# First expert layer: experts sorted by token count on the chip and packed into 14 units of 128 slots

## The chip, the cores and the metric

The kernel runs on one core of a Trainium2 chip. The metric is the device time of one execution in microseconds (us). TensorE (PE) does the matmuls, VectorE (DVE), ScalarE (ACT) and GpSimd (POOL) the elementwise work, and SyncE (SP) issues nearly all transfers. All arithmetic shown here is in f32 or, split into a high and a low part, in fp32r.

## The reference

The program is a block of two transformer layers on 256 latent and 256 context tokens of width 1024, followed by a second block. Each of the two layers ends in a mixture of 32 experts, of which every token takes two. The change touches the first layer's mixture alone, with 512 tokens and so 1024 (token, expert) pairs. Cut to what matters:

```
grp   = argmax(h @ w_group + b_group)                 # one of 4 groups
top_i = the 2 best of the 8 experts of that group
gate  = p_group * softmax over the two
counts[e] = how many tokens take expert e
y[t]  = sum over its two experts e of
        gate * ((silu(h[t] @ w1[e]) * (h[t] @ w3[e])) @ w2[e])
```

w1[e] and w3[e] are 1024 x 512, w2[e] is 512 x 1024, all f32: 2 MiB each, 6 MiB an expert, 192 MiB a layer. The result must not depend on how tokens are laid out for the experts.

## The kernel before, in words

`moe(l, Tn, ob)` is the mixture of layer l over Tn tiles of 128 tokens (4 in the first layer). It routes, ranks each token inside its expert (`pk`), and gives it a slot: `slot = 64 * expert + rank`. Tokens with a rank of 64 or more (`ovr`) go to slots behind `OVF` = 2048.

The main loop at the end of `moe` goes through 16 units of 128 slots, each two experts with 64 slots. For a unit it does, on TensorE: on every second unit `gather` (the tokens of two units are picked by one-hot matrices from `onehot_tok` into `xt`, 8 x 256 columns), `up` with w1 (L1155: for each of 8 rows of weights, one matmul for each expert, 64 stationary columns of `xt` and 512 moving columns of the weight), `trans` of the unit before, `up` with w3, `down` of the unit before (L1190), and `combine` of the unit before (L1217: the result is scattered back to the tokens by one-hot matrices from `scatter_mats` and added to X). An f32 matmul is two matmul instructions, two passes over its 512 columns. Two matmuls with 64 stationary columns, one for each expert of a unit, lie side by side in the array.

Weights come as tiles of 1 MiB through a ring of eleven buffers (`Stream`, `W.load`, L259). One expert is six tiles, the layer 192. The order is that of use: w1 and w3 of unit i+1 before w2 of unit i. SP issues each load as soon as the tile eleven places ahead has been used. The first four experts have fixed places (`FIX`); the number of each of the other 28 is read by SP from the tile `eid` (`Q.value_load`, L820), because places can be swapped at run time.

The swap: `overflow_slots` counts the tokens of each expert (L1101) and works out which have more than 64; `swap` puts one such expert into place 15, the second expert of unit `px` = 7, and unit 7 carries an extra set of 128 slots for its tokens behind the 64th. For this, `up` and `down` take `extra`: each row of that expert's weights is also multiplied with 128 more columns (L1158, L1194); `gather(onehot_tok(swap_base()), 128)` fetches the tokens, and the set has its own `trans`, `scaled` and `combine` (`late`). If more is left, `overflow_loop` (L1265 on) runs a loop with a trip count known only at run time; each trip loads one expert and does 128 slots, with nothing beside it. The branch stands after unit 14.

On the inputs that are used the counts of the first layer, by expert, are 10, 35, 25, 26, 21, 15, 45, 31, 32, 23, 26, 37, 32, 27, 31, 22, 40, 62, 42, 48, 29, 65, 29, 43, 28, 26, 34, 35, 20, 26, 18, 41. Expert 21 has one token more than 64.

Instructions are placed by the tile framework's scheduler, which goes by data dependences and the order in which they are written; on each engine the order is then fixed.

Behind the layer comes the attention of the second layer (its first TensorE work is L397); the modulation projections, spread over several stages, use four matmuls of 32 stationary columns side by side (L314).

Of the kernel before, what the change touches and what calls it, by code (L numbers as in the profile page):

```python
# [19 lines left out]
NE = 32  # L20
# [5 lines left out]
SLOT_FREE = -1.0e6  # L26


def _consts():
# [19 lines left out]
    put("w8", np.broadcast_to((8 - np.arange(8))[None, :], (128, 8)))  # L49
    put("half", np.stack([p < 64, p >= 64], 1))  # L50
# [75 lines left out]
def build(tc, A, out, stages=("A0", "M0", "A1", "M1", "F", "B"), dbg=None, inject=None):  # L126
# [22 lines left out]
    with es:  # L149
# [40 lines left out]
        def C(name):  # L190
            a, b = C1COLS[name]
            return c1[:, a:b]
# [575 lines left out]
        def moe(l, Tn, ob):  # L768
            N = 128 * Tn
            nC = Tn // 2  # L770
            nj = (N - CAP + 127) // 128
# [41 lines left out]
            nP = NE // 2  # L813
            order = list(range(nP))
            px = 7 if l == 0 else None
            dyn = {}

            def sources(i):
                if i not in dyn:
                    ids = [e if l or e < FIX else Q.value_load(eid[0:1, e:e + 1], min_val=0, max_val=NE - 1) for e in (2 * i, 2 * i + 1)]  # L820
                    dyn[i] = list(zip(*map(expert, ids)))
                return dyn[i]

            ws = {}
            for p, i in enumerate(order + [None]):
                if i is not None:
                    ws[i] = [stream.add(lambda i=i, j=j: sources(i)[j], 2, 8, 4) for j in range(2)]
                if p:
                    b = order[p - 1]
                    ws[b].append(stream.add(lambda b=b: sources(b)[2], 2, 4, 2))  # L830
# [8 lines left out]
            with sbuf(f"ringx{l}", nX, "right") as ringX, ExitStack() as mid, ExitStack() as early, ExitStack() as main:  # L839
# [235 lines left out]
                has = sm(1)  # L1075
                V.memset(has, 0.0)
                if l == 0:
                    eid = lbx[:, 0:32].bitcast(I32)

                def swap():  # L1080
                    it, sw = C("iota32"), t2(M_)
                    hs, hd, e15 = (sw[:, 32 * i:32 * i + 32] for i in range(3))
                    dsum = sw[:, 96:97]
                    q = 2 * px + 1
                    V.tensor_scalar(hs, it, float(FIX), None, op0=OP.is_ge)
                    V.scalar_tensor_tensor(hs, ovb[:, 0], 0.0, hs, op0=OP.is_equal, op1=OP.mult)
                    V.scalar_tensor_tensor(hs, ovb[:, 1], 0.0, hs, op0=OP.is_gt, op1=OP.mult, accum_out=has)
                    V.tensor_scalar(hd, it, -1.0, float(q), op0=OP.mult, op1=OP.add)
                    V.scalar_tensor_tensor(hd, hd, 1.0, hs, op0=OP.mult, op1=OP.mult, accum_out=dsum)
                    V.tensor_scalar(e15, it, float(q), dsum, op0=OP.is_equal, op1=OP.mult)  # L1090
                    V.tensor_add(hd, hd, it)
                    V.tensor_sub(hd, hd, e15)
                    V.tensor_copy(eid[0:1], hd[0:1])
                    pick(ek, hd[:, None, None, :].to_broadcast(wide))
                    V.tensor_scalar(ek, ek, float(CAP), None, op0=OP.mult)
                    V.tensor_add(slot, ek, pk)

                def overflow_slots():
                    pc = PS()
                    for t in range(Tn):  # L1100
                        T.matmul(pc[0:32, 0:2], at_[:, t], C("ones")[:, 0:2], start=(t == 0), stop=(t == Tn - 1))  # L1101
                    V.tensor_copy(cntc[0:32], pc[0:32, 0:1])
                    for j in range(nj):
                        V.tensor_scalar(cmp_[0:32, j:j + 1], cntc[0:32], float(CAP + 128 * j), None, op0=OP.is_gt)
                    V.tensor_reduce(ovc[0:32], cmp_[0:32], axis=AX.X, op=OP.add)
                    yield
                    po = PS()
                    for i, m in enumerate(("tri", "ident", "ones")):
                        T.matmul(po[:, 32 * i:32 * i + 32], ovc[0:32].to_broadcast([32, 128]), C(m)[0:32, 0:32], start=True, stop=True)
                    V.tensor_copy(ovb, po[:, 0:96].rearrange("p (a b) -> p a b", a=3))  # L1110
                    V.tensor_sub(ovb[:, 0], ovb[:, 2], ovb[:, 0])
                    V.tensor_sub(ovb[:, 0], ovb[:, 0], ovb[:, 1])
                    if l == 0:
                        swap()
                    pick(bk, ovb[:, 0, None, None, :].to_broadcast(wide))
                    V.tensor_scalar(bk, bk, 128.0, float(OVF - CAP), op0=OP.mult, op1=OP.add)
# [30 lines left out]
                def up(off, ws, mid=lambda: None, extra=False):  # L1147
                    ps = PS()
                    px_ = PS() if extra else None
# [26 lines left out]
                def down(hT_, ws, gt, end=False, extra=None):  # L1176
# [10 lines left out]
                    for k in range(4):  # L1187
                        for jo, ps in enumerate(pss):
                            for q, w in enumerate(ws):
                                T.matmul(ps[m * q:m * q + m, :], hT_[:, k, m * q:m * q + m],  # L1190
                                         at(w, k)[k, slice(512 * jo, 512 * jo + 512)], start=(k == 0), stop=(k == 3))
                        if extra:
                            for jo, ps in enumerate(extra[1]):
                                T.matmul(ps, extra[0][:, k], w[k, slice(512 * jo, 512 * jo + 512)], start=(k == 0), stop=(k == 3))  # L1194
# [60 lines left out]
                def swap_base():  # L1255
                    sb = M_.tile([128, 1], F32, name="sb", tag="sb", bufs=1)
                    V.tensor_scalar(sb, has, -4.0 * OVF, 5.0 * OVF, op0=OP.mult, op1=OP.add)
                    return sb

                def overflow_loop():  # L1260
                    ctr = sm(1)
                    V.tensor_copy(ctr, has)
                    nb = M_.tile([1, 1], I32, name="nb")
                    V.tensor_scalar(nb, ovb[0:1, 2, 0:1], has[0:1], 0.0, op0=OP.subtract, op1=OP.max)
                    nbv = nc.values_load(nb[0:1, 0:1], min_val=0, max_val=2 * N // (CAP + 1))  # L1265
# [11 lines left out]
                pend = late = sr = gt = None  # L1277
                for i in order + [None]:
                    ext = i is not None and i == px
                    after = pend and pend[4]  # L1280
                    if i is not None:
# [3 lines left out]
                        if ext:  # L1285
                            gather(onehot_tok(swap_base()), 128)
# [6 lines left out]
                        if not late and i > 1:  # L1293
                            sr, gt = scatter_mats(swap_base() if after else 128 * i, i == order[-1])
                        if i != 0:
                            p1 = up(off, ws[i][0], extra=ext)
# [4 lines left out]
                        if late:  # L1301
                            combine(late[0], scaled(late[1], late[2]))
                            late = None
                            sr, gt = scatter_mats(128 * i)
                    tr = trans(pend[0]) if pend else None
                    if after:
                        xs = trans(after), [PS(), PS()]
                    if i:
                        p3 = up(off, ws[i][1], extra=ext)
                    if pend:  # L1310
                        ys = down(tr, pend[1], pend[2], i is None, xs if after else None)
                    if i is not None:
                        hx = act(p1[1], p3[1]) if ext else None
                        hd = act(p1[0], p3[0]) if ext else act(p1, p3)
# [4 lines left out]
                    if after:  # L1319
                        late = sr, xs[1], gt  # L1320
                        sr, gt = scatter_mats(128 * i)
                    pend = None if i is None else [hd, ws[i][2], gt, sr, hx]
# [762 lines left out]
```

## Time and profile before

| | us |
|---|---|
| median of three runs | 2151.06 (2144.14 to 2153.21) |
| span of the profiled execution | 2151.6 |
| TensorE busy in it | 2024.5 (94%) |
| DVE, ACT, POOL busy | 1131.6, 675.4, 511.6 |
| bytes moved | 585.43 MB, mean 272 GB/s |

The page gives no time of the profiled execution beside its span. Shares of busy time are means over stages with different limits: the two expert layers, attention, projections and the second block. What counts for a change in one stage is what bounds that stage.

### The profile page before, as it was taken

Reading aid. Unit: us, or ns where it says so; the run is one execution under the profiler, and the core shown is the slowest. Engines: PE = TensorE matmul, PEld = TensorE weight load, DVE = VectorE, ACT = ScalarE, POOL = GpSimd, SP = SyncE. Lnnn points to the kernel's source line nnn. Section 1 sums busy time; section 2 is a strip of 40 time slices with the busy share of each in tenths; the row PEclk is TensorE's granted clock in tenths of the full one; section 3 lists DMA queues with packets and bytes.
Section 4 is the critical chain, followed back from the end, with each engine's and each line's share of the span. In section 5 each row is a group of like instructions: output and inputs, shape, how many; then the busy total and the mean of one; then the engine's idle time right before and its main releaser. Section 6 shows DMA issues by size and latency. Waiting matters only on the chain. (4 is left out here: it accounts for less than half of the span.)

```text
span 2151.6 us, 29161 instructions
## 1 busy us (share of the span) xinstructions
PE 2024.5 (94%) x11233; PEld 1296.2 (60%) x11233; DVE 1131.6 (53%) x2024; ACT 675.4 (31%) x1220; POOL 511.6 (24%) x391
## 2 busy tenths in 40 slices
PE   6999989999999997999889999899989999997998
PEld 3755665445434543567754444343358998997996
DVE  3486574556355446764763333332365885455553
ACT  3365531101001111533731111110145344445553
POOL 1234321223222211420011111111113350242331
PEclk8999999999999999999999999899999999998999
DMA  9572358999689997744359999999964453554552
GB/s 316 210 254 102 98 195 328 419 419 398 235 330 371 421 413 283 256 168 155 119 221 415 424 424 423 388 424 424 424 255 138 137 187 120 193 179 140 184 194 98
DMA packets 154175, 585.43 MB, mean 272 GB/s; under 512 B 17256, under 2 KB 21862, under 8 KB 121134
## 3 DMA queue, kind: packets, MB, share of 16 engines
q1 hardware_dynamic: 153182, 583.48, 70.4%
q8 instruction: 91, 1.49, 0.3%
q14 instruction: 54, 0.44, 0.1%
q10 hardware_dynamic: 848, 0.01, 0.0%
HBM read 582.34 MB, written 1.11 MB: 271 GB/s over the span
## 5 line engine op out<-in xcount | busy, mean ns | idle before, releaser
L1155 PE MATMUL ps<-w,xt 128*64 128x512 f32 x1968 | 474.2, 605 | 16.8 <-DVE sid L1132 11.4
L1155 PEld LDWEIGHTS ps<-w,xt 128*64 128x64 f32 x1968 | 146.3, 139 | 286.8 <-issue 274.8
L1224 POOL TENSOR_TENSOR X<-X,tm 128x512 f32<-128x512 f32 x94 | 128.9, 1372 | 760.6 <-DVE tm L1223 754.8
L226 DVE TENSOR_TENSOR spl<-w,sph 128x1024 fp32r<-128x1024 f32 (+1 forms) x153 | 203.1, 1330 | 197.5 <-ACT sph L223 196.5
L223 ACT CAST sph<-w 128x1024 fp32r<-128x1024 f32 (+1 forms) x204 | 213.0, 1045 | 286.2 <-PE pj L217 255.0
L1208 DVE SCALAR_TENSOR_TENSOR t<-ps,gt,t 128x512 fp32r<-128x512 f32 x62 | 46.5, 751 | 471.9 <-ACT t L1207 469.7
L1190 PE MATMUL ps<-w,t 128*64 128x512 f32 x1000 | 242.6, 596 | 6.5 <-DMA w<-expert_w 5.2
L216 PE MATMUL pj<-hT2h,sph 128*128 128x256 f32 x864 | 241.1, 283 | 0.0
L217 PE MATMUL pj<-hT2l,sph 128*128 128x256 f32 x864 | 240.7, 280 | 0.0
L218 PE MATMUL pj<-hT2h,spl 128*128 128x256 f32 x864 | 239.4, 281 | 0.1
L226 POOL TENSOR_TENSOR spl<-w,sph 128x1024 fp32r<-128x1024 f32 (+1 forms) x51 | 126.5, 2480 | 320.1 <-ACT sph L223 317.8
L1207 ACT ACTIVATE t<-ps,gt 128x512 fp32r<-128x512 f32 x62 | 42.6, 687 | 504.5 <-PE ps L1190 501.1
L1190 PEld LDWEIGHTS ps<-w,t 128*64 128x64 f32 x1000 | 89.4, 137 | 146.4 <-issue 132.4
L217 PEld LDWEIGHTS pj<-hT2l,sph 128*128 128x128 f32 x864 | 163.0, 189 | 0.8 <-issue 0.7
L216 PEld LDWEIGHTS pj<-hT2h,sph 128*128 128x128 f32 x864 | 162.4, 189 | 1.4 <-issue 0.7
L218 PEld LDWEIGHTS pj<-hT2h,spl 128*128 128x128 f32 x864 | 161.8, 189 | 0.4 <-DVE spl L226 0.3
L1217 PE MATMUL ps<-t,sr 128*128 128x512 f32 x400 | 115.3, 419 | 18.6 <-DVE t L1208 13.8
L1223 DVE TENSOR_TENSOR tm<-ps,s 128x512 f32<-128x512 f32 x188 | 123.1, 681 | 10.8 <-PE ps L1217 9.2
L1217 PEld LDWEIGHTS ps<-t,sr 128*128 128x128 f32 x400 | 72.4, 190 | 74.3 <-ACT t L1207 24.5
L1224 DVE TENSOR_TENSOR X<-X,tm 128x512 f32<-128x512 f32 x94 | 100.2, 1066 | 2.0
L402 PEld LDWEIGHTS ps<-c,t 128*128 128x128 f32 x516 | 58.4, 141 | 53.8 <-issue 21.0
L402 PE MATMUL ps<-c,t 128*128 128x128 f32 x516 | 80.2, 281 | 5.7 <-DVE oTl L1481 2.2
(508 smaller groups left out, 3537.6 us busy)
## 6 DMA issues: line engine op xcount, KB each, us to landing
w<-expert_w SPq DMA_DIRECT2D x371, 1024.0 KB
w<-ada_w SPq DMA_DIRECT2D x48, 1024.0 KB
w<-w_in SPq DMA_DIRECT2D x30, 1024.0 KB
X<-expert_w SPq DMA_DIRECT2D x13, 1024.0 KB
w<-diff_w_in SPq DMA_DIRECT2D x12, 1024.0 KB
w<-w_gate SPq DMA_DIRECT2D x12, 1024.0 KB
w<-w_ff_down SPq DMA_DIRECT2D x11, 1024.0 KB
w<-w_ff_gate SPq DMA_DIRECT2D x10, 1024.0 KB
```

Of the source, the lines that this page charges most:

```text
L216: T.matmul(o, l.hi, r.hi, start=start, stop=False, **kw)
L217: T.matmul(o, l.hi, r.lo, start=False, stop=False, **kw)
L218: T.matmul(o, l.lo, r.hi, start=False, stop=stop, **kw)
L223: pin(S.copy(d.hi, src), pinned)
L226: eng.tensor_tensor(d.lo, src, d.hi.bitcast(F32), op=OP.subtract)
L402: T.transpose(o, i, ident[:i.shape[0], :i.shape[0]])
L1155: T.matmul(ps[m * q:m * q + m, :], xt[:, k, off + m * q:off + m * q + m], at(w, k)[k], start=(k == 0), stop=(k == 7))
L1190: T.matmul(ps[m * q:m * q + m, :], hT_[:, k, m * q:m * q + m], at(w, k)[k, slice(512 * jo, 512 * jo + 512)], start=(k == 0), stop=(k == 3))
L1208: V.scalar_tensor_tensor(yl, ps, gt[:, 0:1], yh.bitcast(F32), op0=OP.mult, op1=OP.subtract)
L1217: T.matmul(ps, sr[:, 128 * t:128 * t + 128], ys[jo][q], start=(q == 0), stop=(q == 1))
L1223: V.tensor_mul(tmp, ps, grow[:, t // 2, cs])
L1224: (G if jo else V).tensor_add(X[:, t, cs], X[:, t, cs], tmp)
```

## The change

There are now 14 units in the first layer. The experts are sorted by their token count on the chip. `_plan` lays the units out by rank: three kinds, pairs with 64 slots each (8 pairs by rank and the 2 fixed ones), two units with 32 slots for a rare expert and 96 for one of the two commonest, and two units of four experts with 32 slots each. A unit is always four lanes of 32 columns or two of 64; in a 32+96 unit three of the four lanes use the same weights. `_places` makes a table of each rank's first slot and number of slots, which goes into the constants. `sort_experts` ranks the counts with small matmuls and comparisons and fills `eid` and the table by expert (`tabs`). What goes beyond an expert's places goes to the overflow loop as before. The swap and the extra set are gone. The branch to the loop stands after unit 12 of 14.

```diff
+def _plan():
+    last = NE - FIX - 1
+    big, small, mid = [0, 1], [last, last - 1], list(range(2, NE - FIX - 2))
+    quads = [mid[-4:], mid[-8:-4]]
+    mid = mid[:-8]
+    pairs = [mid[i:i + 2] for i in range(0, len(mid), 2)]
+    units = [(64, [e, e + 1], [0, 1]) for e in range(0, FIX, 2)]
+    kinds = "QPPSPQPPSPPP"
+    for kind in kinds:
+        if kind == "Q":
+            units.append((32, [FIX + r for r in quads.pop(0)], [0, 1, 2, 3]))
+        elif kind == "S":
+            units.append((32, [FIX + small.pop(0), FIX + big.pop(0)], [0, 1, 1, 1]))
+        else:
+            units.append((64, [FIX + r for r in pairs.pop(0)], [0, 1]))
...
-            order = list(range(nP))
-            px = 7 if l == 0 else None
+            order = list(range(len(units)))
...
+            def eid_at(q):
+                r = q - FIX
+                return Q.value_load(eid[0:1, r:r + 1], min_val=0, max_val=NE - 1)
...
-                    ws[i] = [stream.add(lambda i=i, j=j: sources(i)[j], 2, 8, 4) for j in range(2)]
+                    ws[i] = [stream.add(lambda i=i, j=j: sources(i)[j], len(units[i][1]), 8, 4) for j in range(2)]
...
+            for i in order:
+                ws[i] = [[w[j] for j in units[i][2]] for w in ws[i]]
...
+                def sort_experts():
+                    T_ = C("tab")
+                    ones, idn = C("ones"), ident[0:32, 0:32]
+                    V.tensor_scalar(key[0:32], cntc[0:32], T_[0:32, 2:3], T_[0:32, 3:4], op0=OP.mult, op1=OP.add)
+                    pr = PS()
+                    T.matmul(pr[0:32, 0:32], key[0:32].to_broadcast([32, 32]), idn, start=True, stop=True)
+                    V.tensor_scalar(gt_[0:32], pr[0:32, 0:32], key[0:32], None, op0=OP.is_lt)
+                    pr = PS()
+                    T.matmul(pr[0:32, 0:32], ones[0:32, 0:32], gt_[0:32], start=True, stop=True)
+                    T.matmul(pr[0:32, 32:34], gt_[0:32], ones[0:32, 0:2], start=True, stop=True)
+                    V.tensor_scalar(oh[0:32, 0], pr[0:32, 0:32], C("pcol")[0:32], None, op0=OP.is_equal)
+                    V.tensor_scalar(oh[0:32, 1], C("iota32")[0:32], pr[0:32, 32:33], None, op0=OP.is_equal)
+                    pr = PS()
+                    T.matmul(pr[:, 0:32], C("pcol")[0:32].to_broadcast([32, 128]), oh[0:32, 1], start=True, stop=True)
+                    for i in range(2):
+                        T.matmul(pr[:, 32 + 32 * i:64 + 32 * i], T_[0:32, i:i + 1].to_broadcast([32, 128]), oh[0:32, 0], start=True, stop=True)
+                    T.matmul(pr[0:32, 96:98], oh[0:32, 0], T_[0:32, 1:2].to_broadcast([32, 2]), start=True, stop=True)
+                    V.tensor_copy(eid[0:1], pr[0:1, 0:32])
...
                     V.tensor_copy(cntc[0:32], pc[0:32, 0:1])
+                    if l == 0:
+                        sort_experts()
+                        V.tensor_sub(cntc[0:32], cntc[0:32], capc[0:32])
+                    else:
+                        V.tensor_scalar(cntc[0:32], cntc[0:32], float(CAP), None, op0=OP.subtract)
...
-                        if extra:
-                            T.matmul(px_, xt[:, k, 0:128], w[k], start=(k == 0), stop=(k == 7))
-                    return (ps, px_) if extra else ps
+                    return ps
...
-                        if ext:
-                            gather(onehot_tok(swap_base()), 128)
...
-                    if i == (14, 8)[l]:
+                    if i == (12, 8)[l]:
                         stream.ahead(RN + n2)
                         overflow_loop()
```

One argument of the program's construction is new as well: `dynamic_dma_scratch_size=1024`.

## Rows read from the trace of the kernel before

**Rows 1.** The page's 40 slices of the span: TensorE, transfers, GB/s.
```profile
PE   6999989999999997999889999899989999997998
...
DMA  9572358999689997744359999999964453554552
GB/s 316 210 254 102 98 195 328 419 419 398 235 330 371 421 413 283 256 168 155 119 221 415 424 424 423 388 424 424 424 255 138 137 187 120 193 179 140 184 194 98
```

**Rows 2.** Busy time by stretch: stretch, length, engines, granted clock, DMA share, GB/s.
```profile
342.00:382.00 40.00, 39.72 (x222) 21.69 (x220) 27.87 (x72) 5.96 (x10) 10.32 (x9) 1.00 1.02 423
382.00:442.00 60.00, 59.43 (x298) 28.83 (x296) 33.27 (x53) 7.24 (x12) 15.78 (x13) 1.00 1.01 420
526.00:642.00 116.00, 113.38 (x485) 48.90 (x486) 57.67 (x91) 11.56 (x21) 32.10 (x24) 0.97 0.74 289
642.00:702.00 60.00, 59.42 (x298) 27.80 (x296) 35.08 (x56) 7.24 (x12) 15.95 (x13) 1.00 0.91 369
762.00:822.00 60.00, 52.12 (x254) 25.93 (x252) 26.53 (x38) 6.66 (x11) 10.64 (x8) 0.94 0.98 402
342.80:837.00 494.20, 480.86 (x2310) 226.53 (x2308) 257.28 (x432) 56.19 (x95) 120.20 (x92) 0.99 0.93 377
390.00:410.00 20.00, 19.71 (x90) 8.34 (x88) 8.43 (x12) 1.86 (x3) 2.54 (x2) 1.00 1.01 425
1180.00:1290.00 110.00, 108.85 (x516) 46.58 (x514) 39.49 (x72) 14.49 (x24) 14.74 (x12) 1.00 1.02 424
1290.00:1400.00 110.00, 99.16 (x439) 42.60 (x436) 37.07 (x70) 13.90 (x23) 12.84 (x11) 0.94 0.98 406
```

**Rows 3.** Who waited for whom, 342 to 837: total us, times, longest.
```profile
PE ps L1155 <- DVE sid L1132: 7.3, 1, 7.3
...
SPq L259 <- PE ps L1155: 266.9, 53, 17.6
SPq L259 <- PE ps L1190: 64.9, 28, 5.1
```

**Rows 4.** Timeline of TensorE, 677 to 747: start, length, line, operation.
```profile
678.69 7.04 PE L1190 MATMUL ps<-w,t 128*64 128x512 f32 x32
...
704.71 7.09 PE L1190 MATMUL ps<-w,t 128*64 128x512 f32 x32
...
738.73 7.09 PE L1190 MATMUL ps<-w,t 128*64 128x512 f32 x32
```

**Rows 5.** Timeline of TensorE, 450 to 537: unit 3, then unit 7.
```profile
454.50 7.09 PE L1190 MATMUL ps<-w,t 128*64 128x512 f32 x32
...
534.25 1.13 PE L1158 MATMUL ps<-w,xt 128*128 128x512 f32 x2
```

**Rows 6.** Timeline of TensorE, unit 7 and the modulation projections: two lanes, four lanes.
```profile
533.24 1.08 PE L1155 MATMUL ps<-w,xt 128*64 128x512 f32 x4
...
911.40 1.07 PE L314 MATMUL ad<-w,scT 128*32 128x512 f32 x8
```

**Rows 7.** Timelines of DVE and TensorE, 332 to 347: counts and swap.
```profile
333.04 0.15 DVE L1102 COPY s<-ps 32x1 f32<-32x1 f32 x1 [12.45 <-PE ps L1101]
...
343.43 0.85 PE L1109 MATMUL ps<-c,s 32*128 32x32 f32 x6
...
344.32 0.26 DVE L1110 COPY s<-ps 128x96 f32<-128x96 f32 x1 [10.60 <-PE ps L1109]
...
346.47 0.17 DVE L1093 CAST lbx<-t 1x32 int32<-1x32 f32 x1
```

**Rows 8.** Line L820: duration ns min/median/max, first and last start.
```profile
L820 SPq TENSOR_LOAD <-lbx x28: 262/266/283, 346.9 to 368.7; - x28
```

**Rows 9.** Timelines of SP and TensorE at the layer's start and end.
```profile
338.32 31.93 SPq L259 DMA_DIRECT2D w<-expert_w  x18
...
823.62 7.99 SPq L259 DMA_DIRECT2D w<-expert_w  x5
...
860.93 3.55 PE L397 MATMUL ps<-c,R 128*64 128x4 f32 x32
```

More of the change, by code (lines that the diff above doesn't have):

```diff
@@ L25, with _places @@
 FIX = 4
-SLOT_FREE = -1.0e6
+def _plan():
[13 more added lines that the diff above has]
+            units.append((64, [FIX + r for r in pairs.pop(0)], [0, 1]))
+    return units
+UNITS = [_plan(), [(64, [e, e + 1], [0, 1]) for e in range(0, NE, 2)]]
+def _places():
+    tab = np.zeros((128, 4), np.float32)
+    for u, (m, pos, lanes) in enumerate(UNITS[0]):
+        for i, q in enumerate(pos):
+            r = q - FIX if q >= FIX else NE - FIX + q
+            tab[r, 0] = 128 * u + m * lanes.index(i)
+            tab[r, 1] = m * lanes.count(i)
+    for e in range(NE):
+        tab[e, 2:4] = (0, -1 - e) if e < FIX else (NE, NE - 1 - e)
+    return tab
 def _consts():
@@ L770, in moe @@
             nC = Tn // 2
-            nj = (N - CAP + 127) // 128
+            units = UNITS[l]
+            nj = (N - 32 + 127) // 128
             nX, nZ, nY = ((2, 0, 5), (2, 1, 5))[l]
@@ L1074, in moe @@
                 cntc, ovc, cmp_, ovb = sm(1), sm(1), sm(nj), sm(3, 32)
-                has = sm(1)
-                V.memset(has, 0.0)
                 if l == 0:
                     eid = lbx[:, 0:32].bitcast(I32)
[L1080 to L1096, printed above, removed]
@@ L1113, in overflow_slots @@
                     if l == 0:
-                        swap()
-                    pick(bk, ovb[:, 0, None, None, :].to_broadcast(wide))
-                    V.tensor_scalar(bk, bk, 128.0, float(OVF - CAP), op0=OP.mult, op1=OP.add)
+                        bx = gt_
+                        V.tensor_scalar(bx, ovb[:, 0], 128.0, float(OVF), op0=OP.mult, op1=OP.add)
+                        V.tensor_sub(bx, bx, tabs[:, 1])
+                        pick(ek, tabs[:, 0, None, None, :].to_broadcast(wide))
+                        pick(ovr, tabs[:, 1, None, None, :].to_broadcast(wide))
+                        V.tensor_tensor(ovr, pk, ovr, op=OP.is_ge)
+                        V.tensor_add(slot, ek, pk)
+                        pick(bk, bx[:, None, None, :].to_broadcast(wide))
+                    else:
+                        pick(bk, ovb[:, 0, None, None, :].to_broadcast(wide))
+                        V.tensor_scalar(bk, bk, 128.0, float(OVF - CAP), op0=OP.mult, op1=OP.add)
                     V.tensor_sub(bk, bk, ek)
@@ L1145, in scatter_mats, with up @@
                     return sr, gt[:, 2]
-                def up(off, ws, mid=lambda: None, extra=False):
+                def up(off, ws, mid=lambda: None):
                     ps = PS()
-                    px_ = PS() if extra else None
                     m = 128 // len(ws)
@@ L1174, in trans, with down @@
                     return hT_.rearrange("p (c s) -> p c s", c=4)
-                def down(hT_, ws, gt, end=False, extra=None):
+                def down(hT_, ws, gt, end=False):
                     zs = []
@@ L1275, in overflow_loop @@
                             V.tensor_scalar(ctr, ctr, 1.0, None, op0=OP.add)
-                pend = late = sr = gt = None
+                pend = sr = gt = None
+                last = order[-1]
                 for i in order + [None]:
-                    ext = i is not None and i == px
-                    after = pend and pend[4]
                     if i is not None:
@@ L1292, in moe @@
                             next(ov, None)
-                        if not late and i > 1:
-                            sr, gt = scatter_mats(swap_base() if after else 128 * i, i == order[-1])
+                        if i > 1:
+                            sr, gt = scatter_mats(128 * i, i == last)
                         if i != 0:
-                            p1 = up(off, ws[i][0], extra=ext)
+                            p1 = up(off, ws[i][0])
                         if i == 1:
@@ L1300, in moe @@
                             sr, gt = scatter_mats(128)
[L1301 to L1304, printed above, removed]
                     tr = trans(pend[0]) if pend else None
-                    if after:
-                        xs = trans(after), [PS(), PS()]
                     if i:
-                        p3 = up(off, ws[i][1], extra=ext)
+                        p3 = up(off, ws[i][1])
                     if pend:
-                        ys = down(tr, pend[1], pend[2], i is None, xs if after else None)
+                        ys = down(tr, pend[1], pend[2], i is None)
                     if i is not None:
-                        hx = act(p1[1], p3[1]) if ext else None
-                        hd = act(p1[0], p3[0]) if ext else act(p1, p3)
+                        hd = act(p1, p3)
                     if pend:
@@ L1318, in moe @@
                         combine(pend[3], ys, i is None)
[L1319 to L1322, printed above, removed]
-                    if i == (14, 8)[l]:
+                    pend = None if i is None else [hd, ws[i][2], gt, sr]
+                    if i == (12, 8)[l]:
                         stream.ahead(RN + n2)
```

26 lines of the change are left out of this document (11 added, 15 removed).

## The prediction

> **What bounds the kernel now.** I read the slices of the page first, then the busy time by stretch, then who waits for whom, then the timelines. The slices (counted from 0, 53.8 us each) show that the first expert layer, slices 6 to 15, is one of two places where the transfers run at 420 GB/s, and that inside it they fall to 235 and 330 GB/s in slices 10 and 11 while TensorE stays full [rows 1]. The stretches say the same in numbers: TensorE is busy 59.4 of 60 us with transfers at 420 GB/s (382 to 442), 113.4 of 116 us with transfers at 289 GB/s (526 to 642) [rows 2]. So in the second stretch the transfers have room and TensorE has none. The waits agree: between 342 and 837 TensorE's longest wait is one of 7.3 us and no wait of it for a weight transfer stands in the list, while the queue that issues the weight loads waited 266.9 + 64.9 us for TensorE to finish with a ring slot [rows 3]. TensorE sets the pace of this layer; the transfers are just behind it: in the regular part both are full.
>
> **The change part by part.**
>
> *Two units fewer.* A unit's down-projections start at 678.69, 704.71 and 738.73 [rows 4]: 26.0 us without a gather, 34.0 with one, 60.04 per two units. Sixteen units become fourteen: 60.0 us of TensorE less.
>
> *The extra set goes.* From the down-projections of unit 3 (454.50) to those of unit 9 (678.69) are 224.2 us where three regular pairs take 180.1 [rows 4, 5]. The second set of 128 slots thus costs 44.1 us: 48 matmul passes over all 128 columns (L1158, L1194: 16 rows of weights going up and 8 half-rows going down, two passes each), its gather, its own transposes and combine. All of it goes, since the swap is gone too. Together TensorE has 104.1 us less to do.
>
> *Four lanes of 32 in place of two of 64, in four of the units.* Per row of weights four matmuls are issued where there were two. The kernel has this form already, in the modulation projections: eight matmuls of 128*32 over 512 columns take 1.07 us, and four of 128*64 take 1.08 us [rows 6]. Both are two passes; a pass costs 0.43 us whether two or four lanes share it. I cost it at nothing. The other end would be lanes that take turns two by two: 48 passes in each of four units twice over, 48 x 0.43 x 4 = 82.6 us. The row is the same operation with the same kind of moving tile, so I take the low end and keep the other as a rival.
>
> *The weights stay.* All 32 experts are still loaded, 192 tiles of 1 MiB. Their unbroken run of issues begins at 338.32, and the last five are issued from 823.62 to 831.61 [rows 9]; I let the transfers' stretch begin and end some 5 us later, for the way of a tile. In it, 342.8 to 837.0, they moved 494.2 us x 377 GB/s = 186.3 MB [rows 2], 178 of the 192 tiles. At the 424 GB/s of 1180 to 1290, a stretch in which they are full all the time, these bytes take 439.4 us, at the 420 of 382 to 442 they take 443.6 [rows 2]. So the transfers can give back 54.8 or 50.6 us, and no more, whatever TensorE saves. This is late next, and it is the smaller of the two sums: of TensorE's 104 us about 50 come back as waits for weights. They will sit at the two units of four experts: these want 24 tiles in the 30 us in which a unit passes on average, which is 59 us of transfer, and the ring holds 11 tiles. The pairs and the 32+96 units want 12 tiles, 29.7 us at 424, in 30.0 us: there the two stay level and the transfers don't pause. I take the middle, 52.7.
>
> *The pause at the overflow loop stays.* At the branch TensorE stands 7.3 us [rows 3] and the stretch around it, 762 to 822, moves 402 GB/s [rows 2]: 60 x (1 - 402/424) = 3.1 us of transfer lost. The branch keeps its place two units ahead of the end, where the transfers now count: minus 3.1.
>
> *Sorting.* Removed: about a dozen small DVE operations of the swap between 344.32 and 346.47 [rows 7]. Added: as many of them, and some ten small matmuls in three turns between TensorE and DVE. Six such instructions (L1109) take 0.85 us [rows 7], so twenty about 2.8 us of TensorE. Wait added: 0 to 5 us, with the chain behind the up-projections of unit 0 in TensorE's queue and SP's loads of the expert numbers behind the chain; behind those stand all further weight loads. What covers it: the numbers are first wanted by the 21st tile, they now arrive at 346.5, the 28 loads of them run until 368.7 between weight issues [rows 7, 8], and the transfers were full meanwhile (423 GB/s from 342 to 382 [rows 2]). The chain begins earlier than the swap (counts at 333.04, swap after 344.32), so I expect the numbers between 340 and 350. I take 1 us; if the cover is gone, 5. The 28 loads stay 28.
>
> *Off the path.* Three sets less of scatter matrices, combine and gathers on DVE, ACT and POOL (busy 257, 56 and 120 of 494 us [rows 2]): nothing waits for them. The two lines that change in the second layer move one subtraction.
>
> *The end.* From the end of that stretch, 837.0, to the next layer's first TensorE work at 860.93 [rows 9] are 24 us. The last three units are pairs as before, so these stay.
>
> Sum: 52.7 - 3.1 - 1 = 48.6 us. The profiled execution has a span of 2151.6 us, 0.5 above the median of the runs, 2151.06: 2151.06 - 48.6 = 2102.5, I say 2102.
>
> [...] What the rows show: in 1290 to 1400, which contains waits, the granted clock is 0.94 and the transfers move 406 GB/s, against 1.00 and 424 in the stretch before [rows 2]. [...]
>
> The bound from rows alone: had the whole layer the 406 GB/s of that stretch, 186.3 MB would take 458.9 us, a gain of 35.3, less 3.1 and 5: 27.2, or 2124. The other end is 425 GB/s (390 to 410 [rows 2]) with nothing lost: 55.8, or 2095.
>
> **The rivals.**
>
> *The transfers are the bound already.* 420 GB/s in most of the layer speaks for it, and the removal of TensorE work would then change nothing: 2151. Against it are the 289 and 369 GB/s of 526 to 702 [rows 2] and the queue's 331.8 us of waiting for slots [rows 3].
>
> [...]
>
> *Four lanes take turns.* The 82.6 us would come on TensorE. In the two units of four experts half of it hides in waits; I count back 104.1 - 82.6 = 21.5 us saved, of which some 11 us of waits at these units remain: gain about 10, or 2141. For it: four moving tiles at a time instead of two, in runs of 64 where the rows have runs of eight. Against it: rows 6.
>
> *The slots overflow.* A sorted place holds 96, 64 or 32 tokens, and one token more sends the expert through the loop, a full pass that nothing overlaps. Its price: the load of one expert, 6.3 MB at 424 GB/s, 14.8 us, up to that plus an extra set (44.1) and the branch (7.3), 66 us. It decides from the first trip: 2102 + 66 = 2168, slower. What speaks against it is the routing that the reference computes on its inputs: sorted counts of 65 and 62 (96 places), 48 down to 28 (64 places), 27 down to 20 and 18, 15 (32 places), and 10, 35, 25, 26 for the four fixed experts (64 places). The nearest is 27 of 32. The 65 is what the extra set serves today.
>
> **How the numbers follow.** The forecast has 0.83: from 2124 down to 2095, and to 2088 since the fastest of the three runs shown lies 7 us under their median. Transfers already the bound 0.04, lanes in turns 0.08, overflow 0.05. A measurement of this kernel can tell about 0.5%, 10.8 us, from no change. Faster by more: 0.83 and half of the lanes' 0.08: 0.87. Within: the other half and 0.04: 0.08. Slower: 0.05. The range from 2088 to 2124 is the likeliest case's own; the rivals lie outside it.
>
> **What would show each step.** Right: L1158 and L1194 are gone, L1155 comes in two tile forms, 128*64 and 128*32, at the same 0.43 us a pass; TensorE's waits for expert weights appear, some 45 to 55 us in all, nearly all at the third and eighth unit and the one after each; transfers stay at 415 GB/s or more from 343 until the branch; the last expert tile lands near 788 and the next layer starts near 812; everything behind it keeps its length. Wrong: transfers below 400 GB/s with TensorE waiting (a ring too short, or numbers that come late), passes of 0.86 us in the 128*32 form, DMA from inside the loop, or a later stage that gives the time back.

## The result, and the profile after

The changed kernel takes 2114.69 us (median of 4 runs, 2109.43 to 2116.59) against 2150.14 before (2144.14 to 2153.21); the ratio is 0.9835, interval 0.9814 to 0.9856. That is 35 us saved where 48.6 were forecast. The profiled execution after has a span of 2107.6 us and a time of 2109.43, the fastest of its four, while the span of before, 2151.6, can belong only to the slowest of its three, 2153.21, so the two spans show the gain too large.

The slices of the page of after (40 slices of 52.7 us; each row is explained at [rows 1]):

```profile
PE   6999999999899988999889999899989999997997
...
PEclk7999999999999999999999999899999999998999
DMA  8673348999999996633389999999964453554552
GB/s 308 213 258 121 100 171 328 399 414 417 417 414 415 417 373 248 243 139 140 101 354 416 416 417 416 379 417 416 414 239 148 134 187 124 186 181 138 196 197 98
```

The hole of 235 and 330 GB/s that the first expert layer had [rows 1] is gone: the transfers are full from slice 8 to 13. But "full" now reads 414 to 417, and so it does from slice 21 to 28 (but one), the second expert layer, which the change hardly touches and which had 424 in most of its slices. By stretch (columns as in [rows 2]; the first line is the expert layer, the second a stretch of the second layer that answers to 1180 to 1290 before):

```profile
339.00:795.40 456.40, 426.64 (x2296) 185.42 (x2294) 206.76 (x338) 45.20 (x75) 93.27 (x72) 0.97 1.00 408
...
1135.00:1245.00 110.00, 108.85 (x514) 46.40 (x512) 39.50 (x72) 14.48 (x24) 14.75 (x12) 1.00 1.02 416
```

In both stretches of the second layer TensorE is equally busy (108.85 of 110) and the DMA engines equally (1.02); only the bytes moved in that time differ, 424 and 416 GB/s. The single packets say why. Their durations in the records of the trace, hardware queue, second layer (mean of some 3600 and 4000 packets; "most" is the value or the values that most of them have):

```
            8192-byte packets          4096-byte packets
before      309.1 ns, most 309         159.4 ns, most 159
after       315.2 ns, most 313 to 320  163.2 ns, most 159 to 166
```

Who waited in the first expert layer of after, 339 to 796 (total us, times, longest; PEld is TensorE's weight load):

```profile
PEld ps L1210 <- DMA w<-expert_w: 26.4, 16, 3.0
PEld ps L1243 <- DMA w<-expert_w: 17.6, 17, 1.6
...
PE ps L1210 <- DMA w<-expert_w: 13.1, 10, 2.1
...
PE ps L1210 <- DVE sid L1188: 7.3, 1, 7.3
...
PE ps L1243 <- DMA w<-expert_w: 5.9, 10, 0.7
```

Waits of TensorE for weights, of which there were none [rows 3], have appeared; the 7.3 us at the branch has stayed. L1210 and L1243 are the up- and down-projections, L1155 and L1190 before. TensorE's timeline of after, around the first unit of four experts:

```profile
378.58 7.08 PE L1210 MATMUL ps<-w,xt 128*32 128x512 f32 x64
...
392.17 1.05 PE L1210 MATMUL ps<-w,xt 128*32 128x512 f32 x2 [1.38 <-DMA w<-expert_w]
395.34 1.61 PE L1210 MATMUL ps<-w,xt 128*32 128x512 f32 x2 [2.12 <-DMA w<-expert_w]
...
424.45 7.85 PE L1210 MATMUL ps<-w,xt 128*64 128x512 f32 x32
432.23 3.44 PE L1243 MATMUL ps<-w,t 128*32 128x512 f32 x8
436.32 1.90 PE L1243 MATMUL ps<-w,t 128*32 128x512 f32 x4 [0.66 <-DMA w<-expert_w]
438.89 4.46 PE L1243 MATMUL ps<-w,t 128*32 128x512 f32 x24 [0.66 <-DMA w<-expert_w]
...
479.97 7.09 PE L1243 MATMUL ps<-w,t 128*64 128x512 f32 x32
...
506.11 7.14 PE L1243 MATMUL ps<-w,t 128*64 128x512 f32 x32
...
692.25 7.14 PE L1243 MATMUL ps<-w,t 128*64 128x512 f32 x32
```

Two things are read here. The 64 matmuls of 128*32 at 378.58, eight rows of weights and so sixteen passes in four lanes, take 7.08 us, the 32 of 128*64 in two lanes, sixteen passes too, 7.09: a pass is 0.44 us either way. And the idle times in brackets are only part of what a wait costs. The better measure is the time from one unit's down-projections to the next, against the 34.0 us with a gather and 26.0 without that [rows 4] give (479.97 to 506.11 is 26.1):

```
from unit      0     1     2     3     4     5     6     7     8     9    10    11   sum without 11
after       44.2  28.6  47.7  26.1  34.2  45.0  35.8  33.2  37.9  26.2  34.9  36.2
too long    10.2   2.6  13.7   0.1   0.2  19.0   1.8   7.2   3.9   0.2   0.9  10.2   59.8
```

Units 2 and 7, counted from 0, are the two of four experts. TensorE loses 26.5 us at the first of them and its neighbours, 31.9 at the second and its neighbours, next to nothing elsewhere; the 10.2 at the end is the branch, which cost 8.9 before by the same measure. TensorE's idle records for weights (the two PE lines above) show only 19.0 of the 59.8 us. The rest lies under matmuls that are counted as busy: the weight loads (PEld) waited 26.4 + 17.6 = 44.0 us for weights, and a small part is matmuls at a granted clock of 0.50 (at most 6.9 us, as is worked out where the prediction is gone through). How the 59.8 us divide between the two was not measured.

The stages of the profiled executions, cut at the first up-projection of the first layer, the next layer's first TensorE work (860.93 before, [rows 9]), and the first and last up-projection of the second layer. They hold the kernels of the experiments too, which come next. M1 is the second expert layer, from its first to its last up-projection; the part ahead of the first layer, 320 to 326 us, has no column:

```
                                   first layer   attention    M1    rest    span
before                                   536.0       255.4  442.7   592.7  2151.6
before again                             535.9       255.4  440.6   591.5  2147.7
after                                    496.0       255.3  447.0   587.8  2107.6
after again                              495.3       253.9  450.7   590.8  2113.9
three of four experts loaded             465.0       254.8  447.6   588.4  2080.7
before without the extra set             491.3       257.2  441.2   592.6  2106.4
before, tiles 32 bytes lower             533.0       253.9  448.2   592.5  2147.8
after, tiles at 64-byte multiples        492.6       253.9  447.9   592.4  2108.6
  the same, late unit of four            488.8       251.1  448.9   587.1  2098.1
  the same, 15 units                     506.0       257.1  448.7   587.8  2123.7
after, tiles at 256-byte multiples       491.4       255.4  443.8   587.7  2101.9
  the same, late unit of four            481.7       250.9  442.0   591.5  2090.0
  and a ring of 12                       478.7       251.8  442.4   592.6  2091.3
after at 256 bytes, 16 units             496.3       257.2  440.9   592.6  2107.6
```

The first layer lost 40.0 us of its 536.0, not the forecast 48.6, and M1 became 4 to 10 us longer.

### The profile page after: what moved, and what is told of

Read it like the earlier page. It is cut to its first block, busy times and chain, and to the rows that moved or that the text cites. A ratio compares the mean times of both kernels' runs of the same rounds, so it can differ in the third digit from the quotient of the medians.

```text
span 2107.6 us, 28929 instructions
## 1 busy us (share of the span) xinstructions
PE 1961.4 (93%) x11203; PEld 1242.9 (59%) x11203; DVE 1084.2 (51%) x1942; ACT 665.0 (32%) x1200; POOL 484.5 (23%) x371
## 5 line engine op out<-in xcount | busy, mean ns | idle before, releaser
L1210 PE MATMUL ps<-w,xt 128*64 128x512 f32 (+1 forms) x2096 | 455.6, 611 | 29.3 <-DMA w<-expert_w 17.9
L1210 PEld LDWEIGHTS ps<-w,xt 128*64 128x64 f32 (+1 forms) x2096 | 136.4, 133 | 295.2 <-issue 256.9
L1258 DVE SCALAR_TENSOR_TENSOR t<-ps,gt,t 128x512 fp32r<-128x512 f32 x56 | 41.9, 751 | 479.7 <-ACT t L1257 478.2
L1274 POOL TENSOR_TENSOR X<-X,tm 128x512 f32<-128x512 f32 x82 | 111.3, 1358 | 751.4 <-DVE tm L1273 750.2
L1243 PE MATMUL ps<-w,t 128*64 128x512 f32 (+1 forms) x1064 | 254.5, 598 | 15.0 <-DMA w<-expert_w 13.5
L262 POOL TENSOR_TENSOR spl<-w,sph 128x1024 fp32r<-128x1024 f32 (+1 forms) x51 | 126.8, 2485 | 321.5 <-ACT sph L259 319.1
L1243 PEld LDWEIGHTS ps<-w,t 128*64 128x64 f32 (+1 forms) x1064 | 86.2, 130 | 171.7 <-issue 134.2
L1267 PE MATMUL ps<-t,sr 128*128 128x512 f32 x352 | 103.5, 424 | 18.2 <-DVE t L1258 14.9
L1273 DVE TENSOR_TENSOR tm<-ps,s 128x512 f32<-128x512 f32 x164 | 107.3, 681 | 9.7 <-PE ps L1267 9.1
L1267 PEld LDWEIGHTS ps<-t,sr 128*128 128x128 f32 x352 | 64.5, 193 | 69.5 <-ACT t L1257 23.8
L1274 DVE TENSOR_TENSOR X<-X,tm 128x512 f32<-128x512 f32 x82 | 88.4, 1078 | 1.8
```

What stands on the lines that cost most here:

```text
L262: eng.tensor_tensor(d.lo, src, d.hi.bitcast(F32), op=OP.subtract)
L1258: V.scalar_tensor_tensor(yl, ps, gt[:, 0:1], yh.bitcast(F32), op0=OP.mult, op1=OP.subtract)
L1267: T.matmul(ps, sr[:, 128 * t:128 * t + 128], ys[jo][q], start=(q == 0), stop=(q == 1))
L1273: V.tensor_mul(tmp, ps, grow[:, t // 2, cs])
L1274: (G if jo else V).tensor_add(X[:, t, cs], X[:, t, cs], tmp)
```

## The experiments

Each group of runs shared one chip and runs of the kernel before; ratios are to those.

**Group 1.** Is the lower rate the execution's or the change's? Do the transfers set the waits? What is the packing worth?

*The kernel before, unchanged.*

> The kernel before, unchanged, for its trace on the same chip as the runs beside it. The trace of after showed 416 GB/s in the full stretch of the second expert layer, which the change does not touch, where the trace of before had 424. Theory 'the rate belongs to the execution or the chip': this run shows the same rate there as the run of after beside it, within 2 GB/s, whichever rate that is. Rival 'the change lowers the rate': this run shows 424 again and the run of after 416.

Measured: 2149.47 us; 424 GB/s in 1180 to 1290, packets of mostly 309 ns.

*The changed kernel, unchanged.*

> The changed kernel, unchanged, beside the kernel before on one chip. Theory 'rate of the execution': 35 to 48 us below before; the higher the rate in the second expert layer, the more (2.46 us a tile at 424 GB/s, 2.52 at 416: about 6 us less over the layer by an arithmetic of ring and tiles). Rival 'the change lowers the rate': 44 us below before with 416 GB/s here and 424 in the run of before.

Measured: 2115.61 us beside 2148.29, ratio 0.9854 (0.9828 to 0.9880). It moves 415 GB/s in the second layer while the kernel before, on the same chip, moves 424. The rate comes with the change, so my theory (it belongs to the execution) fell. Neither had the time: the theory gave 35 to 48 us below before, the rival 44, and 33 were measured.

*Two experts' weights left out.*

> After, but the two units of four experts load only three experts; the fourth lane uses the weights of the third. Left out: the weights of two experts, 12 tiles of 1 MiB. TensorE issues the same matmuls. Theory 'transfers set the waits at the units of four': 12 x 2.52 = 30 us below after, 26 to 31, near 2085, and TensorE's lost time at these units and the next falls from 60 to about 30 us. Rival 'the waits come from the four lanes, from late numbers or from the slow clock': within 8 us of after.

```
- ids = [q if l or q < FIX else eid_at(q) for q in units[i][1]]
+ ids = [q if l or q < FIX else eid_at(q) for q in units[i][1][:3]]
...
+ ws[i] = [[w[min(j, 2)] for j in units[i][2]] for w in ws[i]]
```

Measured: 2086.89 us, ratio 0.9720 (0.9696 to 0.9744), 28.7 below after, with TensorE's matmuls all there. TensorE's waits for weights, 339 to 796:

```profile
PEld ps L1243 <- DMA w<-expert_w: 13.3, 14, 1.6
PEld ps L1210 <- DMA w<-expert_w: 9.3, 8, 2.4
...
PE ps L1210 <- DMA w<-expert_w: 4.3, 3, 1.5
...
PE ps L1243 <- DMA w<-expert_w: 4.0, 7, 0.7
```

The time lost between down-projections falls from 59.8 to 29.1 us. With half of the surplus weights of these units gone, half of the lost time is gone, while the lanes and the order of the units are as they were. So the waits at the units of four are for the volume of their weights: shown.

*Before, without the extra set.*

> Before, with 16 pairs as they were, but the second set of 128 slots in unit 7 is left out (its passes, gather, transposes, combine); the one token it served is not computed. All 32 experts are loaded. This is 44.1 us of TensorE less, without the packing. Theory 'the transfers limit what is given back': nearly as much as the whole change, 33 to 44 us below before, since 16 pairs of 30.0 us stand level with 12 tiles of 2.46 to 2.52 us. Rival 'each saved TensorE microsecond counts alike': 44/104 of the gain of the change, about 17 us below before.

```
- ext = i is not None and i == px
+ ext = False
```

Measured: 2108.37 us, ratio 0.9815 (0.9791 to 0.9839): 39.9 below before, and 7.2 us *faster* than the changed kernel beside it. Its TensorE has no wait for weights; the down-projections follow at 26.1 and 34.0 us to the end (timeline of this kernel, L1190 as before; the last line is cut off by the end of the stretch asked for):

```profile
453.72 7.09 PE L1190 MATMUL ps<-w,t 128*64 128x512 f32 x32
...
479.79 7.09 PE L1190 MATMUL ps<-w,t 128*64 128x512 f32 x32
...
513.81 2.74 PE L1190 MATMUL ps<-w,t 128*64 128x512 f32 x11
```

Its first layer is 44.7 us shorter than before, just the 44.1 of TensorE's work that went, and its transfers are then full as well:

```profile
342.80:791.80 449.00, 437.79 (x2176) 212.64 (x2178) 241.01 (x402) 52.43 (x87) 109.02 (x84) 0.99 1.00 415
```

Packing 16 units into 14 takes away 60 us more of TensorE's work, and the changed kernel does not get even what this one gets.

**Group 2.** What lowers the rate? The trace only says that packets take longer. The diff has two edits that reach past the first layer: the descriptor scratch at the foot of each SBUF partition is cut from 16384 to 1024 bytes, and the table `tab` puts 4 columns (16 bytes) into the constants, which lie ahead of the weight ring. The cut is a multiple of 256 bytes; the table, rounded up by the allocator, is 32. The first weight tile begins at byte 43008 of a partition before (168 x 256), at 27680 after (108 x 256 + 32), and most of the others lie a multiple of 256 bytes behind it.

*After, moved back to 64-byte multiples.*

> After, with 8 unused columns (32 bytes a partition) behind the constants, so that the weight tiles' addresses in a partition are multiples of 64 again (27712 where after has 27680; before has 43008). In the traces a weight packet of 8192 bytes takes 309 ns in the kernels built on before and 313 to 320 in those built on after. Theory 'the added table of 16 bytes shifts the weight tiles off a 64-byte boundary, and that lowers the rate': packets of 309 ns again, 423 to 425 GB/s in the full stretch of the second layer, and 4 to 8 us below after, since the waits at the units of four shrink with the time of a tile (2.53 to 2.47 us). Rival 'the smaller descriptor scratch lowers the rate': 416 GB/s stays, time within 2 us of after.

```
+ put("pad", np.zeros((128, 8)))
```

Measured: 2111.71 us, ratio 0.9832 (0.9813 to 0.9851), the same as after within its interval; packets of mostly 312, 313 and 319 ns. The second layer's stretch:

```profile
1135.00:1245.00 110.00, 108.84 (x515) 46.16 (x513) 39.48 (x72) 14.49 (x24) 14.75 (x12) 1.00 1.02 416
```

A boundary of 64 bytes is not it. The rival, the smaller scratch, still stands.

*Before, moved off by 32 bytes.*

> Before, with the descriptor scratch at the foot of each partition cut from 16384 to 16352 bytes, which moves every tile 32 bytes down: the weight tiles then start at 32 modulo 64, as in after. Theory of the 64-byte boundary: 313 to 320 ns a packet, 415 to 417 GB/s in the second layer, and the time 0 to 4 us above before, because the first layer is on TensorE and hides it. Rival 'it is something else in the change': 424 GB/s and the time of before.

```
- nc = bacc.Bacc("TRN2", target_bir_lowering=False, num_devices=1)
+ nc = bacc.Bacc("TRN2", target_bir_lowering=False, num_devices=1, dynamic_dma_scratch_size=16352)
```

Measured: 2152.95 us, ratio 1.0017 (1.0005 to 1.0029); packets of mostly 313 and 320 ns. Nothing but the place of the tiles has changed (the scratch is 32 bytes short of what it was, and the weight tiles begin 32 bytes below a multiple of 256), and the rate is that of after:

```profile
1180.00:1290.00 110.00, 108.56 (x508) 46.15 (x504) 42.18 (x77) 16.31 (x27) 14.77 (x12) 1.00 1.02 417
```

The place matters. It costs this kernel only some 2.5 us. In the stages M1 is longer (448.2 against 440.6 and 442.7) and the first layer, which stands on TensorE, is not (533.0 against 536.0 and 535.9).

*The second unit of four in the last place but one.*

> The aligned kernel with the second unit of four moved from the eighth place to the last but one (order P P Q P P S P P P S P P Q P). Theory 'TensorE waits for transfers at units of four, and what the ring holds at the end of the layer is spent on the next stage, which needs it less': an arithmetic of ring and tiles gives 9 us less than aligned (7 to 9), since the transfers' debt of the late unit is partly never paid; waits move to the last three units. Rival 'the sum of transfers sets the end wherever the units stand': within 2 us of aligned. Rival 'a late wait is paid in full': slower than aligned, up to 10 us.

```
- kinds = "QPPSPQPPSPPP"
+ kinds = "QPPSPPPSPPQP"
```

Measured: 2104.26 us, ratio 0.9798 (0.9781 to 0.9815), 7.4 below the same kernel with the usual order: the theory's figure, though the two intervals touch. Group 3 tries it again.

*15 units.*

> The aligned kernel with 15 units: one unit of four experts instead of two (P P P P P S P P P S P P P Q P), eight others in pairs; a gather more. 30 us more TensorE work, 30 us fewer waits. Theory 'both are level, so a unit more costs nothing where it takes away waits': within 4 us of the aligned order with the late unit of four, 0 to 8 us below aligned. Rival 'TensorE's work still sets the time': 15 to 30 us above aligned.

```
- quads = [mid[-4:], mid[-8:-4]]
- mid = mid[:-8]
+ quads = [mid[-4:]]
+ mid = mid[:-4]
...
- kinds = "QPPSPQPPSPPP"
+ kinds = "PPPSPPPSPPPQP"
...
- if i == (12, 8)[l]:
+ if i == (13, 8)[l]:
```

Measured: 2126.25 us, ratio 0.9890 (0.9872 to 0.9907), 14.5 above the kernel with 14 units at 64-byte multiples: neither theory's figure, and the trace says that the run does not answer the question. With an odd number of units the branch now stands ahead of a unit that begins with a gather, and TensorE waits there three times as long:

```profile
775.08 0.55 PE L1087 MATMUL ps<-gr,hh0h 128*128 128x256 f32 x1 [21.89 <-DVE gr L1076]
```

21.9 instead of 7.3 us is 14.6, as much as the whole difference; but the run also has its only unit of four in the last place but one, so that 15 units would otherwise equal 14 is argued, not shown.

**Group 3.** Is 256 bytes enough? What else is there?

*After, at 256-byte multiples.*

> After, with 56 unused columns (224 bytes a partition) behind the constants: the weight tiles start at multiples of 256 bytes (27904 where after has 27680). Before has multiples of 256 (43008) and 309 ns a packet; the kernels at 32 and at 64 modulo 256 have 311 to 320. Theory 'the boundary that counts is wider than 64 bytes, and 256 is enough': 309 ns a packet, 423 to 425 GB/s in the second layer, 4 to 9 us below after's 2115 (3 from the second layer and block, as the shifted before lost, the rest from shorter waits at the units of four). Rival 'the descriptor scratch of 1024 bytes is the cause in the kernels built on after': 312 to 316 ns as in the kernel at 64, time within 2 us of it (2112).

```
+ put("pad", np.zeros((128, 56)))
```

Measured: 2103.63 us (2100.05 to 2104.90), ratio 0.9779 (0.9764 to 0.9794). Packets of 309 ns (96 in 100 of those of 8192 bytes); the layer and a stretch of the second layer (1135 to 1245 has 421, as the transfers are not full in its first 5 us):

```profile
339.00:795.40 456.40, 428.75 (x2313) 188.37 (x2310) 208.82 (x349) 47.09 (x78) 93.32 (x72) 0.97 1.00 413
1145.00:1255.00 110.00, 108.56 (x510) 46.04 (x506) 41.13 (x75) 16.36 (x27) 14.81 (x12) 1.00 1.02 424
```

The scratch is as small as in after and the rate is back, so the rival fell. The 224 unused bytes are worth 0.9835 - 0.9779 = 0.0056 of 2150, 12 us (from the second run of after, 0.9854, it is 16), more than the 4 to 9 that I expected. The time lost between down-projections is 53.4 us, 6.4 less than after.

*The late unit of four again.*

> The same with the second unit of four in the last place but one, as in the run that gained 7 us at the lower rate. Theory 'the ring's stock at the end of the layer pays for the late unit': 6 to 9 us below the kernel beside it with the usual order; both gains add up to some 2098 to 2100. Rival 'at the higher rate the ring is refilled between the units of four, so that the place no longer counts': within 2 us of it.

Measured: 2092.70 us (2091.86 to 2093.72), ratio 0.9732 (0.9719 to 0.9746), 10.9 below the kernel beside it; somewhat more than expected. Its TensorE waits for the second unit of four at the end of the layer, from 716 to 781; the last tile lands at 789.5 and the next layer starts at 805.60, 9.4 us sooner than in the usual order (815.0). The attention stage is shorter too, 250.9 against 255.4 us (in the first pair 251.1 against 253.9), for no cause found here:

```profile
717.93 3.63 PE L1211 MATMUL ps<-w,xt 128*32 128x512 f32 x28 [1.12 <-DMA w<-expert_w]
...
776.04 1.90 PE L1244 MATMUL ps<-w,t 128*32 128x512 f32 x4 [0.59 <-DMA w<-expert_w]
...
805.60 3.55 PE L434 MATMUL ps<-c,R 128*64 128x4 f32 x32
```

*And a ring of 12 tiles.*

> The same with the late unit, and the ring of weight tiles in the first layer one slot longer (12 instead of 11; the room is there because the change cut the scratch). Theory 'transfers are the limit': one more tile lands before the layer begins, so one tile's time, 2.5 us, less (1 to 3). Rival 'TensorE's work after the last wait is the limit by now': within 1 us.

```
- nX, nZ, nY = ((2, 0, 5), (2, 1, 5))[l]
+ nX, nZ, nY = ((2, 0, 6), (2, 1, 5))[l]
```

Measured: 2091.06 us (2088.22 to 2094.24), ratio 0.9721 (0.9705 to 0.9738). The first layer is 3.0 us shorter in the trace, the median of the whole 1.6, inside the spread: not decided. These two kernels are the fastest of the study, 57 to 59 us below before.

*The packing undone alone, tiles at 256-byte multiples.*

> After, aligned, sorted, without the extra set, but no units of four: 16 units (two of 32+96 in the third and the fifteenth place, the others pairs). This undoes the packing alone: 60 us of TensorE work more than 14 units. Theory 'the two units saved come back as waits and slow clock': within 6 us of the aligned kernel with 14 units, more likely above it (an arithmetic of ring and tiles gives 9 above, the slow clock after the waits takes back some); TensorE without waits for weights. Rival 'packing is what gains': 30 to 60 us above it.

```
- quads = [mid[-4:], mid[-8:-4]]
- mid = mid[:-8]
+ quads = []
...
- kinds = "QPPSPQPPSPPP"
+ kinds = "SPPPPPPPPPPPSP"
...
- if i == (12, 8)[l]:
+ if i == (14, 8)[l]:
```

Measured: 2110.83 us, ratio 0.9817 (0.9802 to 0.9831), 7.2 above 14 units; no wait of TensorE for weights in the layer's list. It is 1 us beyond the 6 that I gave the theory, on its side and far from the rival's 30. So of the 60 us that two units less save on TensorE, 7 reach the time.

Put together: the extra set gone, 39.9 (from the run without it); the packing with its sort, 6 to 8; both, with the tiles at 256-byte multiples, 46.3 (2149.96 - 2103.63); and the shifted tiles take 12 of it back, which leaves 34 to 35.

## Why the prediction came out as it did

The measured time lies inside the stated range, but the forecast of 2102 was 12.7 us low: 8.6 of the 48.6 us are missing in the first layer, and M1 gives back 4 to 10 more. The main cause is one that no term of the sum held, the place of the tiles; with them at 256-byte multiples the same change measures 2103.63. That this is so near to 2102 is in part luck: there, too, the first layer is 44.6 us shorter (536.0 to 491.4), not 48.6. The step "0.5 above the median" set a span beside times; it did no harm, since the forecast starts from the median.

*Right: TensorE's sum, and that the transfers cap the gain.* 104.1 us saved, 59.8 given back in waits, 1.3 more at the branch, 2.4 for the sort: 40.6, and the first layer is 40.0 shorter. That the transfers would not let TensorE's whole saving through was the decisive step, and the two kernels with 16 units and no extra set show it: with 60 us more work on TensorE they stand within 8 us of the kernels with 14. Too strong was "and no more, whatever TensorE saves": with the late unit of four the first layer is 54.3 us shorter than before, and with the ring of 12 it is 57.3. There TensorE follows the transfers more closely at the end: in the first of the two it is 16.1 us from the last tile to the next layer, in place of the 24 that the prediction left fixed.

*Right: the places of the waits.* 58.4 of the 59.8 us are at the third and eighth unit and their neighbours. The amount, 45 to 55, was short by 5 for after and fits the 53.4 of the kernel at 256-byte multiples, if it is taken as time lost between down-projections; the records of idle time show only 19.0. TensorE's granted clock is 0.50 from 395.7 to 402.5, 569.8 to 573.2 and 580.0 to 583.4, right behind waits of 1.4 to 2.1 us at the two units of four. That is 13.7 us, and at half the clock at most 6.9 of the 59.8 us, an estimate from these numbers. The waits themselves are the larger part by far.

*Right: the lanes.* 0.44 us a pass for four lanes, as [rows 6] said; the rival of lanes in turns is out, and so are transfers as the only bound (the time fell) and the overflow (no weight load comes from the loop).

*Wrong: the rate of a tile.* The step "at the 424 GB/s of 1180 to 1290 these bytes take 439.4 us" took a rate from before for a kernel whose tiles lie elsewhere. At 416 GB/s the same 186.3 MB take 447.8 us, 8.4 more. The last expert tile lands at 795.4, not 788, and the next layer starts at 817.48, not 812. The trace of before has most of its tiles at multiples of 256 bytes, so its rows gave no warning.

*Wrong: "everything behind it keeps its length".* M1 takes 447.0 and 450.7 us in the two runs of after, 442.7 and 440.6 before: 4 to 10 us that the prediction gave to nothing, though the second layer's transfers stand full [rows 2] and a rate change must reach it.

*Mis-sized: the sort.* I took 1 us. Unit 0 lasts 2.4 us longer on TensorE (from its first up-projection to its down-projections 37.9 us, 321.5 to 359.45; before 35.5, 325.0 to 360.47); the timeline of after has the chain between two up-projections:

```profile
333.07 0.24 PE L1125 MATMUL ps<-c,s 32*32 32x32 f32 x2
333.64 0.24 PE L1128 MATMUL ps<-s,c 32*32 32x32 f32 x2 [0.33 <-DVE s L1126]
...
334.49 0.37 PE L1133 MATMUL ps<-s,c 32*128 32x32 f32 x2 [0.57 <-DVE s L1131]
...
335.39 7.09 PE L1210 MATMUL ps<-w,xt 128*64 128x512 f32 x32
```

The numbers came sooner than forecast (first load of one at 335.7, before 346.9 [rows 8]), so no weight load was late for them.

*Wrong in size and place: the pause at the branch.* I charged 3.1 us of transfers, and let them run full everywhere else up to there. In after the queue of SP issues nothing from 761.4 to 781.9, and the transfers fall to 193 GB/s from 775 to 785, which at 416 is an estimate of 5.4 us; they also fell to 368 between 369 and 389. In all the 186.3 MB took 456.4 us (339 to 795.4 at 408 GB/s), 8.6 more than the 447.8; so they gave back 494.2 - 456.4 = 37.8 us, not 52.7 less 3.1. But these pauses are not what sets the end: TensorE's units from 9 on are back at 26.2 and 34.9 us, its weight loads wait for weights only 0.7 us in all from 690 to 817, and what counts at the end is its own pause:

```profile
772.28 9.90 PE L1210 MATMUL ps<-w,xt 128*64 128x512 f32 x32 [7.29 <-DVE sid L1188]
...
817.48 3.55 PE L433 MATMUL ps<-c,R 128*64 128x4 f32 x32
```

That pause was there before as well (10.2 against 8.9 us by the measure of down-projections), so the branch costs 1.3 us more than before, not 3.1. From the last tile to the next layer it is 22.1 us in after, near the 24 that I let stand.

## What to carry to other kernels

When TensorE's work is already level with the transfers, taking more work away buys little (here 7 of 60 us). Ask what the transfers can still give back, and try the units that want most bytes near the end, where the stock of the ring is not needed afterwards (here the last place but one: 7 and 11 us). Whatever is added to a pool that lies ahead of the weight tiles moves them: compare the duration of equal packets in a stretch that the change does not touch, before believing any rate, and keep the start of the tiles at a multiple of 256 bytes (worth 12 us here).

## What the runs showed of the hardware

The same 8192-byte packet, loaded from HBM to SBUF, mostly takes 309 ns in the six kernels (seven traces) most of whose weight tiles start at a multiple of 256 bytes in their partition. It mostly takes 313 to 320 ns at 32 bytes beyond or 32 below such a multiple, and mostly 312 to 319 at 64 beyond one. The rates are 424 and 415 to 417 GB/s, with the DMA engines at the same busy share (1.02). In these runs the side that is written moved, the place of the tiles in SBUF: at 32 beyond, the mean packet went from 309.1 to 315.2 ns, 2.0%. Why it takes longer stays open. Whether a multiple of 128 would do was not tried.

The part behind the second layer takes either 587 to 588 or 591 to 593 us, with and without the change, for no cause found here; by it alone two profiled spans can differ by 3 to 5 us.
